# A state-space recurrence turned by its phase for VectorE's scan instruction, and the two sides of SBUF exchanged in the first stage

## The chip, the cores and the metric

The kernel runs on one core of one Trainium2 chip. The metric is the device time of one launch in microseconds, the median of the runs. Three runs of the kernel before took 3642.49, 3650.92 and 3659.8 us. The engines are called as in the profile: PE is TensorE, DVE is VectorE, ACT is ScalarE, POOL is GpSimd, SP is SyncE, which here only issues DMAs. ACT and POOL issue DMAs too, in the order of their own instructions.

## The reference

`reference` computes a first block (three mixers, their output projection and a feed-forward layer) and then a second block of two layers on 256 latent rows `x` and 256 context rows `ctx`, each 1024 wide. Layer 0 applies a chunk mixer and a PEER layer (a product-key lookup of rows of two large tables) to `x` and to `ctx`. Layer 1 applies a state-space mixer to `x`, in which the context takes part, and a PEER layer to `x`. The change lies in the state-space mixer, which is this, cut:

```python
def _diag_scan(a_r, a_i, bu_r, bu_i, h0=None):       # h[t] = a * h[t-1] + bu[t], complex, a is diagonal
    if h0 is not None:
        inj_r, inj_i = _cmul(a_r, a_i, h0[0], h0[1])
        bu_r = bu_r.at[0].add(inj_r)
        bu_i = bu_i.at[0].add(inj_i)
    ...
def _ssm_direction(u_lat, u_ctx, ...):
    hc_r, hc_i = _diag_scan(a_r, a_i, *inject(u_ctx))
    hx_r, hx_i = _diag_scan(a_r, a_i, *inject(u_lat), h0=(hc_r[-1], hc_i[-1]))
    return readout(hx_r, hx_i)
def _ssm_mixer(...):
    mag = exp(lr * step); a_r = mag * cos(li * step); a_i = mag * sin(li * step)
    ...
    y = forward(u_x, u_c) + reversed(backward(u_x[::-1], u_c[::-1]))
    val, gate = split(gelu(y + d_skip * u) @ w_out)
    return val * sigmoid(gate)
```

There is one complex state per group and state index and direction. Only the last state of the context's scan is used; it seeds the scan over the latent rows.

## The kernel before

The program is written in Python, and a scheduler with a simulated timeline sets the order of the instructions on each engine from the data dependences, the sizes of buffers and priorities (`c.low()` marks work that gives way). Tiles of a pool with one side ("left", the default, or "right") are stacked on that side of SBUF; a pool opened later on the same side overlies the memory of one that was closed, and its first writes wait until the last reads there are done.

`tile_block` runs these stages. The prefix (0 to some 345 us) computes four chunks of the modulation (a small matrix product on `cvec`), then side by side the tables of the state-space mixer (`ssm_build`, low priority, pool `sb` on the right), the context's norm and chunk mixer (pool `c0` on the left, with the pool `cm` inside) and the fused keys of layer 0's PEER (`fuse_keys`, pool `fk` on the left; heads 4 to 7 last). After the prefix, pools `sp` and `c1` open on the right (norm of the context for its PEER: the rows `brow`, `nrow` and the token rows `htok`, which POOL adds up), and `b0` on the left for the first block. The context's PEER is gathered row by row by POOL's indirect DMAs under the first block and under the dense PEER layer of `x` (`peer_dense`). Near the end of `peer_dense` the context's half of the state-space mixer runs (`ssm_ctx`), then the latent half (`ssm_mixer`), then layer 1's `peer_dense` and the final norm.

`ssm_build` computes, for 64 state columns on each of 128 partitions, the coefficient a of the state (`ar`, `ai`, from the cosine and sine `hs`, `sn` and the size `mag`), its powers a, a2, a3, a4, then the powers of a4 (call it A) up to the eighth by `cmul` on DVE (six small instructions each, helper `tt`, line 1196), copies of them by ACT into `pt`, and stores `pt` as `ssm_p`. A and its eighth power stay as `A1, A2, B1, B2`. The rest of `ssm_build`, which is left as it is, makes injection matrices `ssm_m`, readout matrices `ssm_g` and within-step matrices `ssm_t` in eight rounds; each round begins with a memset of `ts` by POOL and ends with stores that ACT issues. Because a matrix product takes four time steps at once, 256 rows make 64 steps with coefficient A.

`ssm_inject` multiplies the input by `ssm_m` on PE into four time-series per pair of states (32 pairs, two directions d, real and imaginary r) of 64 steps, copied to `Sx` by ACT. The scan over the 64 steps is then done in three parts: `ssm_local` runs seven steps inside eight blocks of eight (each step four DVE instructions for half a group of pairs, 128 elements per partition), one of four groups on POOL; `ssm_carry` runs seven steps over the blocks; `ssm_apply` (only for the latent rows) multiplies the carried states by the powers in `ssm_p` and adds them, partly on POOL. `ssm_ctx` works on four groups of eight pairs, with loads issued by POOL; `ssm_mixer` likewise, then PE reads out `Hx` with `ssm_g` (line 1598) and `ssm_t` (line 1596).

Lines of helpers: 159 and 166 copy a PSUM bank to SBUF by ACT or DVE, 308 and 315 split a weight tile in two parts by ACT and by DVE or POOL, 227, 251 and 254 are small transposes and row broadcasts on PE, 777 is the matrix product of `peer_dense`, 909 that of `fuse_keys`, 806 and 832 are additions of a modulation and of a residual.

Of the kernel before, what the change touches and what calls it, by code (L numbers as in the profile page):

```python
# [11 lines left out]
F32 = mybir.dt.float32  # L12
# [4 lines left out]
ALU = mybir.AluOpType  # L17
# [1159 lines left out]
def ssm_build(c, pool, sb):  # L1177

    nc, I, tc = c.nc, c.I, c.tc
    A1, A2, B1, B2 = (pool.tile([P, 32, 2, 2], F32, name=n) for n in ("A1", "A2", "B1", "B2"))  # L1180
    pd = c.dram.tile([P, 1024], F32, name="ssm_p")
# [51 lines left out]
    pw = sb.tile([P, 5, 2, W], F32, name="pw")  # L1233
    tt(pw[:, 1, 0], mag, hs, ALU.mult)
    tt(pw[:, 1, 1], mag, sn, ALU.mult)
    ar, ai = pw[:, 1, 0], pw[:, 1, 1]
# [17 lines left out]
    def cmul(ore, oim, xr, xi, yr, yi, w1, w2):  # L1254
        tt(w1, xr, yr, ALU.mult)
        tt(w2, xi, yi, ALU.mult)
        tt(ore, w1, w2, ALU.subtract)
        tt(w1, xr, yi, ALU.mult)
        tt(w2, xi, yr, ALU.mult)
        tt(oim, w1, w2, ALU.add)  # L1260

    for n in (2, 3, 4):
        cmul(pw[:, n, 0], pw[:, n, 1], pw[:, n - 1, 0], pw[:, n - 1, 1], ar, ai, t1, t2)

    pt = sb.tile([P, 32, 2, 2, 8], F32, name="pt")
    nc.gpsimd.memset(pt[:, :, :, :, 0:1], 0.0)
    cur = pw[:, 4]
    for n in range(1, 9):
        if n > 1:
            nx = sb.tile([P, 2, W], F32, tag="pn", name="pn", bufs=2)  # L1270
            cmul(nx[:, 0], nx[:, 1], cur[:, 0], cur[:, 1], pw[:, 4, 0], pw[:, 4, 1], t1, t2)
            cur = nx
        srcs = [cur[:, j].rearrange("p (d q) -> p q d", d=2) for j in range(2)]
        if n < 8:
            for j in range(2):
                nc.scalar.copy(pt[:, :, :, j, n], srcs[j])
        if n in (1, 8):
            X1, X2 = (A1, A2) if n == 1 else (B1, B2)
            for r in range(2):
                nc.scalar.copy(X1[:, :, :, r], srcs[0])  # L1280
                nc.scalar.mul(X2[:, :, :, r], srcs[1], 1.0 - 2.0 * r)
    nc.scalar.dma_start(pd, pt.rearrange("p a d r n -> p (a d r n)"))
# [114 lines left out]
    return dict(a4=(A1, A2), a32=(B1, B2), powers=pd, m=md, g=gd, t=td)  # L1397


def ssm_inject(c, uT, Sx, mats, g, first=0):  # L1400


    for q in range(4 * g, 4 * g + 4):
        m = mats(q).rearrange("p (a j m) -> p a j m", a=2, j=4)
        ps = c.ps()
        for a in range(2):
            for j in range(4):
                c.nc.tensor.matmul(
                    ps[:, (a * 4 + j) * 64 : (a * 4 + j + 1) * 64], m[:, a, j, :], uT[:, 2 * q + a, :], start=True, stop=True
                )  # L1410
        i = 2 * q - first
        c.evac(Sx[:, i : i + 2].rearrange("p a d r j -> p (a d r j)"), ps, eng="a")
# [12 lines left out]
def ssm_local(c, eng, pool, A, Sx, p0, n, tag, first=0):  # L1425

    m = n // 2

    def at(h, j):
        return _view(Sx, (p0 - first + h * m) * 256 + j, [[256, m], [128 + 7 - 2 * j, 2], [64, 2], [8, 8]])

    def step(j, i):

        for h in range(2):
            a = [v[:, p0 + h * m : p0 + (h + 1) * m].unsqueeze(4).to_broadcast([P, m, 2, 2, 8]) for v in A]
            if i < 2:
                t[h][i] = pool.tile([P, m, 2, 2, 8], F32, tag=f"{tag}{i}{h}", name=f"sl{i}", bufs=1)
                eng.tensor_tensor(t[h][i], a[i], at(h, j - 1), ALU.mult)  # L1440
            else:
                v = t[h][0] if i == 2 else _view(t[h][1], 8, [[32, m], [16, 2], [-8, 2], [1, 8]])
                eng.tensor_tensor(at(h, j), at(h, j), v, ALU.add)

    t = [[None, None], [None, None]]
    for j in range(1, 8):
        for i in range(4):
            step(j, i)


def block_view(t, s):

# [12 lines left out]


def ssm_apply(eng, pool, pw, C, Sx, H, p0, n, d, tag):

    shp = [P, n, 2, 8, 7]
    ps = slice(p0, p0 + n)  # L1470
    t1 = pool.tile(shp, F32, tag=tag + "1", name="sa1", bufs=1)
    t2 = pool.tile(shp, F32, tag=tag + "2", name="sa2", bufs=1)
    cb = C[:, ps, d].rearrange("p q r b -> p q (r b)").unsqueeze(3).to_broadcast([P, n, 16, 7])
    for r, t in enumerate((t1, t2)):
        power = _view(pw, p0 * 32 + d * 16 + r * 8 + (1 if d == 0 else 7), [[32, n], [0, 16], [1 - 2 * d, 7]])
        eng.tensor_tensor(t.rearrange("p q r b j -> p q (r b) j"), cb, power, ALU.mult)
    eng.tensor_tensor(t1[:, :, 0], t1[:, :, 0], t2[:, :, 1], ALU.subtract)
    eng.tensor_tensor(t1[:, :, 1], t1[:, :, 1], t2[:, :, 0], ALU.add)
    hv, sv = (t[:, ps, d].rearrange("p q r (b j) -> p q r b j", b=8) for t in (H, Sx))
    o, i = (slice(1, 8), slice(0, 7)) if d == 0 else (slice(0, 7), slice(1, 8))  # L1480
    eng.tensor_tensor(hv[:, :, :, :, o], t1, sv[:, :, :, :, i], ALU.add)


def ssm_ctx(c, mats, modT, ctx, last, pool):
# [3 lines left out]
    hT = pool.tile([P, KD, S], F32, tag="big", name="chT", bufs=2)  # L1488
# [27 lines left out]
    ends = pool.tile([P, 32, 2, 2, 8], F32, name="ends")  # L1516
    for g in range(4):
        Sx = pool.tile([P, 8, 2, 2, 64], F32, tag="big", name="cSx", bufs=2)
        ssm_inject(c, uT, Sx, lambda q: load(mats["m"][q // 4][:, (q % 4) * 1024 : (q % 4 + 1) * 1024]), g, g * 8)
        pool_too = g in CTX_POOL  # L1520
        ssm_local(
            c, nc.gpsimd if pool_too else nc.vector, pool, mats["a4"], Sx, g * 8, 8, "slp" if pool_too else "slv",
            g * 8,
        )
        for d in range(2):
            sv = Sx[:, :, d].rearrange("p q r (b j) -> p q r b j", b=8)
            nc.scalar.copy(ends[:, g * 8 : (g + 1) * 8, d], sv[:, :, :, :, 0 if d else 7])
    cur = block_view(ends, 0)
    for s in range(1, 8):
        nx = last if s == 7 else pool.tile([P, 32, 2, 2], F32, tag="sst", name="sst", bufs=2)  # L1530
        ssm_carry(c, pool, mats["a32"], block_view(ends, s), cur, nx)
        cur = nx


def ssm_mixer(c, mats, modT, x, last, fill, gate):

    nc, I = c.nc, c.I
    with ExitStack() as out:
# [12 lines left out]
        with c.tc.tile_pool(name="sy", bufs=1) as sy:  # L1551
            Sx = sy.tile([P, 32, 2, 2, 64], F32, name="Sx")
# [17 lines left out]
            nc.scalar.dma_start(pw.rearrange("p a d r n -> p (a d r n)"), mats["powers"])  # L1570

            def at_block(s):
                return block_view(C, s)

            nc.vector.tensor_copy(at_block(0), last)
            for s in range(7):
                e = _view(Sx, 8 * s + 7, [[256, 32], [128 + 49 - 16 * s, 2], [64, 2]])
                ssm_carry(c, sz, mats["a32"], e, at_block(s), at_block(s + 1))
            for d in range(2):
                nc.scalar.copy(H[:, :, d].rearrange("p q r (b j) -> p q r b j", b=8)[:, :, :, :, 7 * d], C[:, :, d])  # L1580
# [339 lines left out]
```

## Time and profile before

| | |
|---|---|
| median of 3 runs | 3650.92 us (3642.49 to 3659.8) |
| the profiled execution's own time | 3635.85 us |
| its span (first to last instruction) | 3634.1 us |
| busy in the span | PE 3284.0, DVE 2640.1, ACT 1402.9, POOL 1338.2 us |
| moved by DMA | 940.44 MB, mean 259 GB/s |
| share of the chain that ended last | PE 57%, DVE 21%, DMA 13% |

The profiled execution is 15 us below the median and 7 us below the fastest of the three runs. The prefix and the two state-space stages are read separately, by windows of 20 or 40 us, because the share of busy time over the whole span hides what limits them.

### The profile page before, as it was taken

The numbers are of one execution on the slowest core, as the hardware profiler recorded it, in microseconds if no ns is written. First come the engines' busy times: TensorE is split into PE (matmuls) and PEld (weight loads), VectorE is DVE, ScalarE is ACT, GpSimd is POOL, SyncE is SP. The second block draws the span as 40 slices with busy tenths as digits, with TensorE's granted clock in tenths as the row PEclk, the third lists the DMA queues.
The fourth block names the chain that finished last, engine by engine and source line by source line (L and its number), as shares of the span: only waits on it lengthen the run. The fifth ranks groups of instructions, "written<-read, shape, count | busy, mean of one in ns | idle before, by whom it ended". The sixth has DMA issues, their size and how long they took to land.

```text
span 3634.1 us, 49746 instructions
## 1 busy us (share of the span) xinstructions
PE 3284.0 (90%) x18136; PEld 2665.8 (73%) x18136; DVE 2640.1 (73%) x5276; ACT 1402.9 (39%) x2586; POOL 1338.2 (37%) x1021
## 2 busy tenths in 40 slices
PE   6996987999889988879999999997589999999998
PEld 4775563747437756678899999976477988999987
DVE  5676986555655568878988888859968987555555
ACT  3553222011310023237444544442133475544454
POOL 0000244444334447448544444414444374001000
PEclk9997998999899999999999999998799999999999
DMA  8875778899588988586998888853554466555553
GB/s 304 288 246 185 280 254 312 336 343 338 211 315 333 355 325 277 178 275 206 357 342 329 338 335 330 336 197 109 199 197 174 163 192 238 209 209 209 209 203 116
DMA packets 280485, 940.44 MB, mean 259 GB/s; under 512 B 22944, under 2 KB 136880, under 8 KB 209200
## 3 DMA queue, kind: packets, MB, share of 16 engines
q1 hardware_dynamic: 142560, 608.22, 46.0%
q0 software_dynamic: 77184, 281.05, 21.2%
q10 hardware_dynamic: 60496, 47.99, 4.0%
q8 instruction: 142, 2.33, 0.2%
q14 instruction: 103, 0.84, 0.1%
HBM read 870.60 MB, written 66.58 MB: 258 GB/s over the span
## 4 chain that ended last, share of the span: by engine, by line
PE 57%; DVE 21%; DMA 13%; issue 4%; POOL 3%; ACT 2%; ACTq 1%; DVEq 0%; POOLq 0%; SPq 0%
PE bank L777 18%; PE bank L350 6%; PE bank L349 6%; PE bank L348 6%; DMA gat<-peer_u_rows,idx 5%; DMA gat<-peer_v_rows,idx 5%; PE bank L364 4%; PE bank L357 4%; DVE spl L315 2%; DVE sl L1440 2%; PE bank L909 2%; POOL o L1102 2%; PE bank L1105 1%; PE bank L337 1%; PE bank L335 1%
## 5 line engine op out<-in xcount | busy, mean ns | idle before, releaser
L315 DVE TENSOR_TENSOR spl<-w,sph 128x1024 fp32r<-128x1024 f32 x552 | 701.9, 1273 | 344.0 <-ACT sph L308 341.8
L308 ACT CAST sph<-w 128x1024 fp32r<-128x1024 f32 x632 | 661.9, 1049 | 558.9 <-PE bank L349 372.6
L350 PE MATMUL bank<-hs,spl 128*128 128x256 f32 x2048 | 582.5, 284 | 6.7 <-DVE spl L315 6.7
L348 PE MATMUL bank<-hs,sph 128*128 128x256 f32 x2048 | 581.0, 284 | 2.0 <-DVE mod L806 1.8
L349 PE MATMUL bank<-hs,sph 128*128 128x256 f32 x2048 | 581.0, 284 | 0.0
L1015 DVE CUSTOM_DVE_ANT_0 gat<-gat,htok 128x1024 f32<-128x1024 f32 x256 | 331.7, 1303 | 177.5 <-DMA gat<-peer_u_rows,idx 154.9
L1027 DVE SCALAR_TENSOR_TENSOR pacc<-gat,act,pacc 128x1024 f32<-128x1024 f32 x256 | 333.8, 1304 | 149.9 <-DMA gat<-peer_v_rows,idx 134.4
L348 PEld LDWEIGHTS bank<-hs,sph 128*128 128x128 f32 x2048 | 392.5, 192 | 11.6 <-ACT sph L308 1.9
L350 PEld LDWEIGHTS bank<-hs,spl 128*128 128x128 f32 x2048 | 392.7, 192 | 10.5 <-DVE spl L315 9.3
L349 PEld LDWEIGHTS bank<-hs,sph 128*128 128x128 f32 x2048 | 392.6, 192 | 8.3 <-issue 0.5
L315 POOL TENSOR_TENSOR spl<-w,sph 128x1024 fp32r<-128x1024 f32 x80 | 201.4, 2518 | 453.5 <-ACT sph L308 436.3
L364 PE MATMUL bank<-hT,w 128*128 128x256 f32 x1472 | 328.6, 384 | 14.1 <-DVE cv L509 8.4
L364 PEld LDWEIGHTS bank<-hT,w 128*128 128x128 f32 x1472 | 283.3, 193 | 64.9 <-issue 11.6
L777 PE MATMUL bank<-sph,wsl 128*128 128x512 f32 x1024 | 318.6, 392 | 2.3 <-DVE wsl L315 2.2
L1000 POOL DMA_INDIRECT gat<-peer_v_rows,idx x176 | 214.2, 1217 | 286.5 <-PE bank L357 61.2
L777 PE MATMUL bank<-spl,wsh 128*128 128x512 f32 x1024 | 319.4, 393 | 0.1
L777 PE MATMUL bank<-sph,wsh 128*128 128x512 f32 x1024 | 307.5, 394 | 2.4 <-ACT wsh L308 2.4
L1000 POOL DMA_INDIRECT gat<-peer_u_rows,idx x176 | 219.1, 1245 | 227.5 <-DVE act L1015 77.9
L357 PE MATMUL bank<-w,hT 128*128 128x512 f32 x576 | 255.6, 603 | 2.2 <-ACT sg L432 2.2
L777 PEld LDWEIGHTS bank<-sph,wsl 128*128 128x128 f32 x1024 | 192.2, 188 | 45.3 <-DVE wsl L315 2.6
L777 PEld LDWEIGHTS bank<-spl,wsh 128*128 128x128 f32 x1024 | 189.8, 188 | 39.8 <-DVE spl L315 0.3
L357 PEld LDWEIGHTS bank<-w,hT 128*128 128x128 f32 x576 | 110.7, 194 | 135.9 <-issue 132.0
(444 smaller groups left out, 5730.3 us busy)
## 6 DMA issues: line engine op xcount, KB each, us to landing
w<-peer_u_t SPq DMA_DIRECT2D x128, 1024.0 KB, 5.6
w<-peer_v_t SPq DMA_DIRECT2D x128, 1024.0 KB, 5.1
w<-ada_w_t SPq DMA_DIRECT2D x48, 1024.0 KB, 6.7
w<-wq_t SPq DMA_DIRECT2D x32, 1024.0 KB, 5.4
w<-w_in_t SPq DMA_DIRECT2D x32, 1024.0 KB, 7.9
gspill<-gstg SPq DMA_DIRECT2D x32, 896.0 KB, 4.6
gq<-gspill SPq DMA_DIRECT2D x28, 1024.0 KB, 6.2
w<-wqk SPq DMA_DIRECT2D x24, 1024.0 KB, 5.3
```

The source lines that it names most:

```text
L308: nc.scalar.copy(hi, src)
L315: eng.tensor_tensor(lo, src, hi.bitcast(F32), ALU.subtract)
L348: mm(ps, wh[:, ks], hh[:, k, :], start=k == 0, stop=False)
L349: mm(ps, wh[:, ks], hl[:, k, :], start=False, stop=False)
L350: mm(ps, wl[:, ks], hh[:, k, :], start=False, stop=k == KD - 1)
L357: m = self.nc.tensor.matmul(outs[t], hT[:, k, t * P : (t + 1) * P], w[k], start=k == 0, stop=k == KD - 1)
L364: m = self.nc.tensor.matmul(ps, block[:, k * P : (k + 1) * P], hT[:, k, :], start=k == 0, stop=k == KD - 1)
L777: c.nc.tensor.matmul(acc[t][cc], a[:, ts_], b[:, cc * 512 : (cc + 1) * 512], start=first and j == 0, stop=last and j == 2,)
L909: nc.tensor.matmul(ps[:, b * P : (b + 1) * P], wv[:, kt, k * P : (k + 1) * P], ks[:, kt, :], start=kt == 0, stop=kt == 1,)
L1000: g = nc.gpsimd.indirect_dma_start(out=gt, out_offset=None, in_=tab, in_offset=bass.IndirectOffsetOnAxis(ap=idx[:, t, s : s + 1], axis=0))
L1015: use = nc.vector.tensor_tensor_reduce(out=gt, in0=gt, in1=h[:, t, :], scale=1.0, scalar=0.0, op0=ALU.mult, op1=ALU.add, accum_out=act[:, ...
L1027: use = nc.vector.scalar_tensor_tensor(acc, gt, act[:, t, s : s + 1], acc, ALU.mult, ALU.add)
```

## The change

**The scan.** The coefficient A of a state is written as its size times a turn, M exp(i w). A state series multiplied at step n by exp(-i w n) obeys a recurrence whose coefficient is the real number M, and that is what VectorE's `tensor_tensor_scan` computes along a row. `ssm_build` makes tables of the phases exp(i w n), n = 0 to 63, for eight groups of four pairs: `square` doubles the angle seven times, and `phases` fills a table in six levels by multiplying what is there with the next doubling; all of it runs on POOL, and ACT issues the store of each table (512 KB). The powers, their copies and `B1, B2` are gone. In `ssm_ctx` and `ssm_mixer`, `ssm_turn` multiplies a group by the conjugate phase (two DVE instructions, two more for sum and difference), four scans follow, and the mixer turns the result back (`ssm_turn` again and four instructions into `Hx`). `ssm_decay` makes the row of M with zeros at the starts (ACT copies, POOL memset). POOL does no other part of the scan. `ssm_ctx` goes in eight groups of four pairs, `ssm_mixer` in four of eight, and in the latter the modulation's later chunks (`fill`) are issued ahead of the scans.

**The sides.** In the prefix `sb` goes to the left, and `c0` with `cm` to the right. So `sp` and `c1` overlie `c0`, and `b0` overlies `sb` and `fk`.

The diff, cut (`ssm_local`, `ssm_carry` and `ssm_apply` are removed whole):

```diff
 def ssm_build(c, pool, sb):
-    for n in (2, 3, 4):
-        cmul(pw[:, n, 0], pw[:, n, 1], pw[:, n - 1, 0], pw[:, n - 1, 1], ar, ai, t1, t2)
...
-    for n in range(1, 9):
-        if n > 1:
...
-            cmul(nx[:, 0], nx[:, 1], cur[:, 0], cur[:, 1], pw[:, 4, 0], pw[:, 4, 1], t1, t2)
...
-    nc.scalar.dma_start(pd, pt.rearrange("p a d r n -> p (a d r n)"))
+    def square(o, cs, si):
+        gp.tensor_tensor(g1, cs, cs, ALU.mult)
+        gp.tensor_tensor(g2, si, si, ALU.mult)
+        gp.tensor_tensor(o[:, 0], g1, g2, ALU.subtract)
+        gp.tensor_tensor(g1, cs, si, ALU.mult)
+        gp.tensor_tensor(o[:, 1], g1, g1, ALU.add)
+
+    square(lv[:, 1], hs, sn)
+    square(lv[:, 0], lv[:, 1, 0], lv[:, 1, 1])
+    for l in range(1, 6):
+        square(lv[:, l], lv[:, l - 1, 0], lv[:, l - 1, 1])
...
+    def phases(k):
+
+        ph = sb.tile([P, 2, 2, 4, 64], F32, tag="ph", name="ph")
+        w = sb.tile([P, 2, 4, 32], F32, tag="phw", name="phw")
+        for cs in range(2):
+            gp.memset(_view(ph, cs * 512, [[256 + 63, 2], [64, 4]]), 1.0 - cs)
+        for l in range(6):
+            L = 1 << l
...
+            for cs in range(2):
+                gp.tensor_tensor(dst[cs], src[0], m[cs], ALU.mult)
+                gp.tensor_tensor(wv, src[1], m[1 - cs], ALU.mult)
+                gp.tensor_tensor(dst[cs], dst[cs], wv, ALU.add if cs else ALU.subtract)
+        nc.scalar.dma_start(pd[k], ph.rearrange("p s d a n -> p (s d a n)"))
+
+    for k in range(8):
+        phases(k)
...
+def ssm_turn(nc, pool, ph, S, n):
+
+    w1, w2 = (pool.tile([P, 2, 2, n * 64], F32, tag=f"sw{i}", name=f"sw{i}") for i in range(2))
+    cs, si = (_view(ph, i * n * 128, [[n * 64, 2], [0, 2], [1, n * 64]]) for i in range(2))
+    nc.vector.tensor_tensor(w1, S.rearrange("p d r a j -> p d r (a j)"), cs, ALU.mult)
+    nc.vector.tensor_tensor(w2, _view(S, n * 64, [[n * 128, 2], [-n * 64, 2], [1, n * 64]]), si, ALU.mult)
+    return w1, w2
...
+def ssm_scan(c, pool, ph, dec, S, n, ini=None):
...
+    w1, w2 = ssm_turn(nc, pool, ph, S, n)
+    flat = S.rearrange("p d r a j -> p d r (a j)")
+    for r in range(2):
+        nc.vector.tensor_tensor(flat[:, :, r], w1[:, :, r], w2[:, :, r], ALU.subtract if r else ALU.add)
+    if ini is not None:
+        o = edge(S, n, False)
+        nc.vector.tensor_tensor(o, o, ini.rearrange("p a d r -> p d r a"), ALU.add)
+    N = n * 64
+    for d in range(2):
+        for r in range(2):
+            s = _view(S, (d * 2 + r) * N + d * (N - 1), [[1 - 2 * d, N]])
+            f = _view(dec, d * N + d * (N - 1), [[1 - 2 * d, N]])
+            nc.vector.tensor_tensor_scan(s, f, s, 0.0, ALU.mult, ALU.add)
...
 def ssm_ctx(c, mats, modT, ctx, last, pool):
+    for h in range(8):
+        p0 = h * 4
+        S_ = pool.tile([P, 2, 2, 4, 64], F32, tag="cSx", name="cSx", bufs=2)
+        ssm_inject(c, uT, S_, lambda q: load(mats["m"][q // 4][:, (q % 4) * 1024 : (q % 4 + 1) * 1024]), p0, 4)
+        ph = load(mats["phase"][h], "cph")
+        ssm_scan(c, pool, ph, ssm_decay(c, pool, mats["m4"], p0, 4), S_, 4)
...
 def ssm_mixer(c, mats, modT, x, last, fill, gate):
+            Sg = {g: inject(g) for g in range(3)}
+            fill(sy)
...
+            for g in range(4):
+                ph = sy.tile([P, 4, 8, 64], F32, tag="ph", name="ph", bufs=2)
...
+                ssm_scan(c, sy, ph, ssm_decay(c, sy, mats["m4"], 8 * g, 8), S_, 8, ini[:, gs])
+
+                w1, w2 = ssm_turn(nc, sy, ph, S_, 8)
+                if g == 0:
+                    Sg[3] = inject(3)
+                H = sy.tile([P, 2, 2, 8, 64], F32, tag="Hx", name="Hx", bufs=2)
...
-    with tc.tile_pool(name="sb", bufs=1, side="right") as sb:
+    with tc.tile_pool(name="sb", bufs=1) as sb:
-        with tc.tile_pool(name="fk", bufs=1) as fk, tc.tile_pool(name="c0", bufs=1) as p:
+        with tc.tile_pool(name="fk", bufs=1) as fk, tc.tile_pool(name="c0", bufs=1, side="right") as p:
-            chunk_mixer(c, p, ch3, xc, lambda g: gate_bcast(c, mod0, 1, 0, g), mid)
+            chunk_mixer(c, p, ch3, xc, lambda g: gate_bcast(c, mod0, 1, 0, g), mid, "right")
```

Line numbers of the kernel after are 3 lower for helpers, and some 18 higher in the rest of `ssm_build`.

ACT's queue in the prefix, the kernel after, at the stores of the seventh and eighth phase table (`ssm_p<-ph`); `mst` and `wqk` belong to the fused key of head 4, `sph<-w` is a split of a weight of the context's chunk mixer:

```order
L156 COPY rep<-mt 128x4x128 x2
L1297 DMA ssm_p<-ph 128x1024
L305 CAST sph<-w 128x1024 x3
L156 COPY mst<-bank_65 128x512
L912 DMA wqk_2008<-mst 128x4x128
L191 ACTIVATE half,ss<-xc 128x512 x2
L912 DMA wqk_2008<-mst 128x4x128
L1297 DMA ssm_p<-ph 128x1024
L156 COPY mst<-bank_62 128x512
```

The kernel before has one store of `ssm_p` in the prefix, and none at this place; ACT's instructions behind each store stand behind POOL's work for that table.

POOL's queue in the prefix, the kernel after, at the end of the seventh table and the beginning of the eighth (`ts` is the memset with which a round of `ssm_build` begins):

```order
L1295 TENSOR_TENSOR phw<-ph,lv 128x256
L1296 TENSOR_TENSOR ph<-ph,phw 128x2x4x32
L1364 MEMSET ts 128x512
L1286 MEMSET ph 128x2x4 x2
L1294 TENSOR_TENSOR ph<-ph,lv 128x2x4 x2
L1295 TENSOR_TENSOR phw<-ph,lv 128x8
L1296 TENSOR_TENSOR ph<-ph,phw 128x2x4
```

The kernel before, the same queue:

```order
L1286 MEMSET mt 128x2048
L1287 MEMSET gb 128x2560
L1346 MEMSET ts 128x512 x8
L1686 ISA
L1686 TENSOR_TENSOR htok<-half,brow 128x512 x4
```

Before, the eight memsets of `ts` stand alone ahead of `htok`; after, 323 multiplications and additions of `square` and `phases` stand among them, and the last two memsets and `htok` behind all of these.

PE's queue at the end of layer 0's `peer_dense`, first before (injections of the context, line 1408, among the last matrix products, line 777):

```order
L777 MATMUL bank_63<-sph,wsl 128x512
L1408 MATMUL bank_68<-cuT,cw 128x64 x8
L1408 MATMUL bank_62<-cuT,cw 128x64 x8
L777 MATMUL bank_64<-sph,wsl 128x512
L777 MATMUL bank_65<-sph,wsh 128x512
L777 MATMUL bank_61<-sph,wsh 128x512
```

and after:

```order
L774 MATMUL bank_65<-sph,wsl 128x512
L1426 MATMUL bank_68<-cuT,cw 128x64 x8
L1426 MATMUL bank_62<-cuT,cw 128x64 x8
L774 MATMUL bank_61<-sph,wsl 128x512
L224 MATMUL bank_66<-ident,mod_105 128x128 x4
L1426 MATMUL bank_68<-cuT,cw 128x64 x8
```

Before, five such pairs of injections stand ahead of the last product of `peer_dense`; after, one pair does and the other seven stand behind it.

DVE's queue in `ssm_ctx`, the kernel after, one group (line 1481 is the scan, four of 256 elements):

```order
L1461 TENSOR_TENSOR sw_11448<-cSx,cph 128x1024
L1462 TENSOR_TENSOR sw_11449<-cSx,cph 128x1024
L193 TENSOR_TENSOR s_18532<-ss 128x2
L1472 TENSOR_TENSOR cSx<-sw_11448,sw_11449 128x2x256 x2
L174 TENSOR_SCALAR rstd<-s_18532 128x2
L1481 SCALAR_TENSOR_TENSOR cSx<-dec,cSx 128x256 x4
```

Eight such groups take the place of 168 instructions of the local scan and 28 of the carry on DVE.

## Rows read from the trace of the kernel before

**Rows 1.** Busy time of the span, from the page.

```profile
PE 3284.0 (90%) x18136; PEld 2665.8 (73%) x18136; DVE 2640.1 (73%) x5276; ACT 1402.9 (39%) x2586; POOL 1338.2 (37%) x1021
```

**Rows 2.** Windows of the prefix: busy us (count), granted clock, DMA share, GB/s.

```profile
160.00:200.00 40.00, 38.31 (x233) 22.44 (x232) 18.08 (x49) 16.61 (x45) 0.00 (x0) 0.93 0.93 363
200.00:240.00 40.00, 36.84 (x213) 29.71 (x213) 31.80 (x69) 20.60 (x44) 1.05 (x2) 0.94 0.53 186
```

**Rows 3.** Timeline of ACT: start, us, instruction, idle before and releaser.

```profile
42.35 0.24 ACT L1230 ACTIVATE hs<-s 128x64 f32<-128x64 f32 x1
247.59 0.59 ACT L159 COPY mst<-bank 128x512 f32<-128x512 f32 x1 [7.84 <-PE bank L909]
338.19 0.34 ACTq L1396 DMA_DIRECT2D ssm_t<-ts  x1
341.39 0.59 ACT L159 COPY brow<-bank 128x512 f32<-128x512 f32 x1 [8.80 <-DMA ssm_t<-ts]
```

**Rows 4.** Timeline of PE at the same place.

```profile
342.03 5.49 PE L251 MATMUL bank<-mod,ident 128*128 128x512 f32 x6 [6.47 <-ACT brow L159]
```

**Rows 5.** Landing of the stores and loads of ssm_p.

```profile
DMA to landing us min/median/max: 7.5/8.5/9.4
```

**Rows 6.** POOL instructions: ns of one, least, median, most.

```profile
L1440 POOL TENSOR_TENSOR sl<-A,cSx x28: 456/610/4684, 2460.6 to 2501.5; 128x128 f32<-128x128 f32 x28
L963 POOL TENSOR_TENSOR eq<-eq,cid x48: 1852/1890/3007, 393.7 to 2904.2; 128x864 f32<-128x864 f32 x48
L1102 POOL TENSOR_SCALAR o<-iota,slots x160: 780/1127/3721, 1600.7 to 3019.3; 128x128 f32<-128x128 f32 x160
```

**Rows 7.** Timeline of POOL and DVE in the routing stage.

```profile
400.65 1.04 DVE L959 TENSOR_TENSOR eq<-ti,iota 128x864 f32<-128x864 f32 x1
401.84 1.88 POOL L963 TENSOR_TENSOR eq<-eq,cid 128x864 f32<-128x864 f32 x1 [2.69 <-DVE eq L959]
402.35 2.28 DVE L959 TENSOR_TENSOR eq<-ti,iota 128x864 f32<-128x864 f32 x1
```

**Rows 8.** DVE in the prefix by form: count, busy us, mean ns of one.

```profile
L315 DVE TENSOR_TENSOR spl<-w,sph 128x1024 fp32r<-128x1024 f32 x24 | 29.1, 1221 | 8.1 <-ACT sph L308 7.9
L1309 DVE TENSOR_TENSOR pb<-w,w 128x256 f32<-128x256 f32 x45 | 18.9, 421 | 10.5 <-ACT mt L1320 9.9
L832 DVE TENSOR_TENSOR xc<-xc,half 128x512 f32<-128x512 f32 x4 | 2.6, 684 | 0.0
L1196 DVE TENSOR_TENSOR s<-pn,pw 128x64 f32<-128x64 f32 x24 | 4.3, 220 | 0.1
```

**Rows 9.** Windows of the state-space stages.

```profile
2560.00:2580.00 20.00, 17.55 (x155) 14.46 (x154) 19.79 (x53) 6.72 (x12) 19.64 (x18) 1.00 0.92 352
2449.10:2674.40 225.30, 151.77 (x1042) 131.31 (x1041) 219.24 (x481) 47.63 (x78) 123.12 (x159) 0.83 0.44 157
```

**Rows 10.** The same of the instructions of local scan (tile sl) alone.

```profile
2440.00:2700.00 260.00, 136.87 (x336) 77.52 (x112) 0.84 0.46 167
```

**Rows 11.** The same of the instructions of carry (tile st) alone.

```profile
2440.00:2700.00 260.00, 17.89 (x56) 0.84 0.46 167
```

**Rows 12.** The same of the instructions of apply (tile sa) alone.

```profile
2440.00:2700.00 260.00, 43.11 (x45) 37.72 (x35) 0.84 0.46 167
```

**Rows 13.** Timeline of PE at the ends of peer_dense and of the readout.

```profile
2467.68 3.68 PE L1408 MATMUL bank<-cuT,cw 128*128 128x64 f32 x32
2472.40 0.63 PE L777 MATMUL bank<-sph,wsl 128*128 128x512 f32 x2
2680.50 0.38 PE L1596 MATMUL bank<-w,suT 128*64 128x128 f32 x2
2680.72 1.04 PE L1598 MATMUL bank<-w,Hx 128*64 128x128 f32 x8
2681.69 2.20 PE L1609 MATMUL bank<-ident,sy 64*128 64x64 f32 x32
```

**Rows 14.** Timeline of DVE at the last apply.

```profile
2673.76 0.62 DVE L1481 TENSOR_TENSOR Hx<-sa,Sx 128x448 f32<-128x448 f32 x1
```

More of the change, by code (lines that the diff above doesn't have):

```diff
@@ L1179, in ssm_build @@
     nc, I, tc = c.nc, c.I, c.tc
-    A1, A2, B1, B2 = (pool.tile([P, 32, 2, 2], F32, name=n) for n in ("A1", "A2", "B1", "B2"))
-    pd = c.dram.tile([P, 1024], F32, name="ssm_p")
+    A1, A2 = (pool.tile([P, 32, 2, 2], F32, name=n) for n in ("A1", "A2"))
+    M4 = pool.tile([P, 32, 2], F32, name="M4")
+    pd = c.dram.tile([8, P, 1024], F32, name="ssm_p")
     md = c.dram.tile([NS // 2, P, NP * 1024], F32, name="ssm_m")
@@ L1232, in ssm_build @@
     nc.vector.tensor_scalar(hs, hs, -2.0, 1.0, ALU.mult, ALU.add)
[L1233 to L1236, printed above, removed]
+    ar, ai = small("ar"), small("ai")
+    tt(ar, mag, hs, ALU.mult)
+    tt(ai, mag, sn, ALU.mult)
     den, am1 = small("den"), small("am1")
@@ L1396, in ssm_build, with ssm_inject @@
         nc.scalar.dma_start(td[:, q * NP * P : (q + 1) * NP * P], ts_.rearrange("p a t m -> p (a t m)"))
-    return dict(a4=(A1, A2), a32=(B1, B2), powers=pd, m=md, g=gd, t=td)
-def ssm_inject(c, uT, Sx, mats, g, first=0):
-    for q in range(4 * g, 4 * g + 4):
+    return dict(a4=(A1, A2), m4=M4, phase=pd, m=md, g=gd, t=td)
+def ssm_inject(c, uT, S, mats, p0, n):
+    for i in range(0, n, 2):
+        q = (p0 + i) // 2
         m = mats(q).rearrange("p (a j m) -> p a j m", a=2, j=4)
@@ L1467, in ssm_apply, with edge @@
[L1467 to L1481, printed above, removed]
+def edge(S, n, last):
+    i = 63 if last else 0
+    return _view(S, i, [[2 * n * 64 + 63 - 2 * i, 2], [n * 64, 2], [64, n]])
@@ L1515, in ssm_ctx @@
             nc.vector.transpose(uT[:, cc * 16 : (cc + 1) * 16, t * 32 : (t + 1) * 32], u)
[L1516 to L1523, printed above, removed]
-        )
[L1525 to L1532, printed above, removed]
+    ends = pool.tile([P, 32, 2, 2], F32, name="ends")
+    eph = pool.tile([P, 2, 32, 2], F32, name="eph")
+    for h in range(8):
[4 more added lines that the diff above has]
+        ssm_scan(c, pool, ph, ssm_decay(c, pool, mats["m4"], p0, 4), S_, 4)
+        nc.scalar.copy(ends[:, p0 : p0 + 4].rearrange("p a d r -> p d r a"), edge(S_, 4, True))
+        for i in range(2):
+            nc.scalar.copy(
+                eph[:, i, p0 : p0 + 4].rearrange("p a d -> p d a"), _view(ph, i * 512 + 63, [[256 - 63, 2], [64, 4]])
+            )
+    t1, t2 = (pool.tile([P, 32, 2, 2], F32, name=f"st{i}") for i in range(2))
+    for t, i in ((t1, 0), (t2, 1)):
+        nc.vector.tensor_tensor(t, ends, eph[:, i].unsqueeze(3).to_broadcast([P, 32, 2, 2]), ALU.mult)
+    for r in range(2):
+        nc.vector.tensor_tensor(
+            last[:, :, :, r], t1[:, :, :, r], t2[:, :, :, 1 - r], ALU.add if r else ALU.subtract
+        )
 def ssm_mixer(c, mats, modT, x, last, fill, gate):
@@ L1570, in ssm_mixer @@
[L1570 to L1580, printed above, removed]
@@ L1583, in ssm_mixer @@
+            nc.vector.tensor_tensor(ini, ini, _view(t2, 1, [[4, 32], [2, 2], [-1, 2]]), ALU.add)
+            y = sz.tile([64, 4, D], F32, name="sy")
             yv = y.rearrange("p t (q m) -> p q t m", m=32)
             tm = c.w(mats["t"], 32)
[L1585 to L1601 removed]
@@ new lines, in ssm_mixer @@
+            for g in range(4):
+                gs = slice(8 * g, 8 * g + 8)
+                ph = sy.tile([P, 4, 8, 64], F32, tag="ph", name="ph", bufs=2)
+                for h in range(2):
+                    nc.scalar.dma_start(
+                        ph[:, :, 4 * h : 4 * h + 4], mats["phase"][2 * g + h].rearrange("p (s a n) -> p s a n", s=4, a=4)
+                    )
+                S_ = Sg.pop(g)
+                ssm_scan(c, sy, ph, ssm_decay(c, sy, mats["m4"], 8 * g, 8), S_, 8, ini[:, gs])
[3 more added lines that the diff above has]
+                H = sy.tile([P, 2, 2, 8, 64], F32, tag="Hx", name="Hx", bufs=2)
+                nc.scalar.copy(edge(H, 8, False), last[:, gs].rearrange("p a d r -> p d r a"))
+                for d in range(2):
+                    for r in range(2):
+                        o, i = (slice(1, 64), slice(0, 63)) if d == 0 else (slice(0, 63), slice(1, 64))
+                        v1, v2 = (w[:, d, r].rearrange("p (a j) -> p a j", a=8)[:, :, i] for w in (w1, w2))
+                        nc.vector.tensor_tensor(H[:, d, r, :, o], v1, v2, ALU.add if r else ALU.subtract)
+                for q in (2 * g, 2 * g + 1):
+                    ps = c.ps()
+                    gm = c.w(mats["g"][q], 2, NP * 512).tiles[0].rearrange("p (a j m) -> p a j m", a=NP, j=4)
+                    for a in range(NP):
+                        pr = q * NP + a
+                        o = ps[:64, a * P : (a + 1) * P]
+                        nc.tensor.matmul(o, uT[:, pr, :], tm[pr], start=True, stop=False)
+                        for j in range(4):
+                            nc.tensor.matmul(
+                                o, H[:, j // 2, j % 2, pr - 8 * g, :], gm[:, a, j, :], start=False, stop=j == 3
+                            )
+                    nc.scalar.activation(
+                        yv[:, q * NP : (q + 1) * NP], ps[:64].rearrange("p (a t m) -> p a t m", a=NP, t=4),
+                        AF.Gelu_apprx_tanh,
+                    )
```

127 lines of the change are left out of this document (42 added, 85 removed).

## The prediction

> **What bounds the kernel now.** I read the page first: PE is busy in 90% of the span and DVE in 73% [rows 1], so over most of the span DVE hides under PE. The reader is to see in the windows that this doesn't hold in the two stretches that the change touches.
>
> In the state-space stages, 2449.1 to 2674.4 us, DVE is busy 219 of 225 us and PE 152 [rows 9]. The recurrence is most of it: 136.9 us of DVE for the local scans [rows 10], 17.9 for the carry [rows 11], 43.1 for the apply [rows 12], 197.9 in all. The remaining 21 us are splits of weights, norms and transposes. PE's readout ends 7.3 us behind DVE's last apply, at 2681.7 [rows 13, 14]. DVE bounds this stretch, and POOL takes a fourth of the scan beside it.
>
> In the prefix no engine is full: DVE 18 to 32 of 40 us, PE 37 to 38, DMA up to 363 GB/s, POOL nothing but memsets [rows 2]. It is a chain over PE, ACT, DVE and stores. At its end ACT's `brow` waits for the last store of `ssm_t`, issued at 338.19, and PE has then stood 6.47 us [rows 3, 4].
>
> **The change in the state-space stages.** A context group has two instructions of 1024 elements, two of 512 and four scans of 256; a mixer group twice two of 2048, two of 1024, four scans of 512, and four of 504. An instruction of two operands in SBUF takes 0.42 us for 256 elements, 0.684 for 512, 1.22 for 1024 [rows 8]. From the last two the slope is 1.05 ns an element, so 2048 take some 2.3 us (an estimate).
>
> What one scan costs no row shows. From below it is such an instruction of its size, 0.42 and 0.684; nothing in it could take less, since it reads and writes the same elements. From above I take an element more of that slope for each element, 0.42 + 0.27 = 0.69 and 0.684 + 0.54 = 1.22. I take the upper end, since each element needs the result of the one before it, which none of these rows has to wait for.
>
> - Context, 8 groups: 2 x 1.22 + 2 x 0.684 + 4 x 0.69 = 6.6 us, 53 in all (44 at the lower end).
> - Mixer, 4 groups: 4 x 2.3 + 2 x 1.22 + 4 x 1.22 + 4 x 0.684 + 0.2 for the start values = 19.5 us, 78 in all (69).
>
> That is 131 us (113) for 197.9: 67 us of DVE gone (85).
>
> [...]
>
> What is given back:
> - In PE's order five pairs of injections stand ahead of the end of `peer_dense` before, and one after. So `peer_dense` ends four of 3.68 us earlier, at 2473 - 15 = 2458 [rows 13], but DVE's first turn can start only there and not at 2449. Some of DVE's other work ahead of it moves earlier too; I count 8 us.
> - The readout of the last group is two quarters of four pairs, at most 8 x 1.42 = 11.4 us [rows 13], where 7.3 now lie behind the last apply: 2 to 4 us. That of groups 0 to 2 lies beside DVE's 19 us for the next group.
> - DMA: 12 MB for the context (8 of matrices, 4 of phases) at 1.5 MB per 6.6 us is 238 GB/s; then phases 4, matrices 8, `ssm_t` 2, `ssm_g` 8 and the modulation 8 MB within some 90 us is 350 GB/s, and the fastest window here has 352 [rows 9]. The modulation stands ahead of `ssm_t` and `ssm_g` on SP's queue, so group 0's readout can come late, and with two buffers of `Hx` DVE would wait for it. I count 5 us, and up to 30 as a bound.
>
> ACT's part (evacuations, `dec`) is a few short copies a group beside DVE's 6.6 us, and POOL, which was busy 123 us here [rows 9], keeps only memsets. So 67 - 8 - 3 - 5 = 51 us are won.
>
> **The change in the prefix.** DVE loses 10 `cmul`, 60 instructions of 0.22 us or less [rows 8], 8 to 13 us, beside other work. POOL gains 323 instructions in one chain: 35 of 64 elements and 8 tables of 6 each at 8, 16, ..., 256 elements.
>
> A POOL instruction takes 0.456 us for 128 elements at the least and 1.852 for 864 [rows 6]: 1.9 ns an element and 0.21 us fixed. A table is then 36 x 0.21 + 6 x 504 x 0.0019 = 13.3 us, `square` 35 x 0.33 = 11.7, together 118 us. Beside a working DVE 128 elements have a median of 0.61 [rows 6], 1.34 times: 158 us. Each table but the last is one buffer whose store must have landed, 8.5 us for 512 KB [rows 5], before the next begins: 60 us. `hs` and `sn` are there at 42.35 [rows 3] and DVE's normalisation takes to some 47. The chain ends at 47 + 158 + 60 = 265 us. Its bounds: 47 + 118 + 50 = 215, and, if each of them took as long over its least as line 1102 does with 128 elements (1.127 to 0.456, 2.5 times [rows 6]), 47 + 290 + 60 = 397.
>
> What waits for it is in ACT's order: the seventh and eighth store stand just around the first `mst` of the fused keys, whose counterpart began at 247.59 [rows 3]. ACT executes in order, so behind the waiting store are queued the copies `mst` that feed PE's line 909, the splits and all later copies of `ssm_build`. At 265 ACT waits some 20 us there (0 at 215, 150 at 397). I put the prefix's delay at 20 us.
>
> Two things beside it. In the routing stage one DVE instruction that takes 1.04 us alone took 2.28 when a POOL instruction was under way, and ended with nothing in between [rows 7]. The prefix has some 160 such DVE instructions with both operands in SBUF (24 of line 315, and 45 each of line 1309 and of its two sisters 1305 and 1308, 29 + 3 x 19 = 86 us [rows 8]), so DVE loses too; its idle time of 8 to 22 us in 40 [rows 2] takes up most of it, and I count 6 us. [...]
>
> The exchange: `c1` no longer waits for `ssm_build`'s memory, so the 6.47 us of PE [rows 4] can go. `brow` is still issued behind `ssm_build`'s last instructions on DVE and ACT, so nothing more than that can. Now `b0` waits for `ssm_build` instead, but its tiles are first written behind the context's norm, so that this is covered.
>
> Prefix: +20 + 6 - 6 = 20 us later. PE's work behind it is a chain through the whole span, so this is not made up.
>
> **Sum.** 20 - 51 = -31 us. Against the profiled execution's 3636 us that is 3605; the median of the runs stands 15 above, so the prediction is 3619 us.
>
> **Rivals.**
>
> 1. *POOL's chain becomes the prefix's bound* and the change is slower. Place: ACT's stores of the phase tables. Price: each us by which the chain ends behind 247 us is a us of delay, up to 150. It decides from where POOL's instructions take 0.75 us in the mean (323 x 0.75 + 60 + 47 = 349, delay 100): then +100 - 51 = +49, 3700 us; from 80 us of delay the gain is gone to beyond 0.5%. For it: the median beside DVE is a third above the least, single ones took 4.7 us [rows 6], and the tables are built from rows of 1 to 32 elements, which no row of POOL shows. Against it: three quarters of the instructions have 64 elements or fewer.
>
> 2. *The scans cost no more than a product*, and the phase chain is done in time. 85 - 16 = 69 won, the prefix at -6 to 0: 3580 us. For it: the bound from below; against it: the dependence from element to element.
>
> 3. *The loads and the hand-overs take the gain.* Phases double what each group waits for; if readout and turns run at the pace of the loads and the whole 30 us are lost, 51 - 25 = 26 are won and the prefix gives 20 back: 3645 us, no change. For it: 350 GB/s needed where the best window has 352 [rows 9]; against it: loads of earlier stages can be ahead.
>
> That the exchange does nothing, because the order keeps `brow` where it was, costs 6 us in each of these.
>
> **How the numbers follow.** The forecast (3595 to 3640) has 0.48, rival 1 0.17, rival 2 0.13, rival 3 0.22. A difference of under 0.5%, 18 us, can't be told from none here; the limits are 3633 and 3669. Faster: 0.85 of the forecast, all of rival 2, 0.3 of rival 3: 0.41 + 0.13 + 0.07 = 0.61. Same: 0.07 + 0.15 + 0.02 of rival 1 = 0.24. Slower: the rest of rival 1, 0.15. The range 3572 to 3672 leaves out most of rival 1 and the far end of rival 2, some 0.2; that of the forecast alone is 3595 to 3640.
>
> **What would show it.** Steps right: the eighth store of `ssm_p` near 265 us with ACT idle ahead of it for POOL; `brow` near 360; DVE rows of scans of 0.69 and 1.22 us; DVE at 19 of 20 us from 2480 on; the readout's end 30 us earlier than 2682. Wrong: POOL's small instructions over 0.7 us (rival 1) or the chain done by 215; scans of 0.42 and 0.68 (rival 2); DVE idle in the mixer behind DMAs or PE (rival 3).

## The result, and the profile after

| | before | after | ratio, 95% interval |
|---|---|---|---|
| first comparison, 4 runs each | 3646.70 us | 3584.79 us | 0.9826 [0.9801, 0.9851] |
| second, 9 and 5 runs | 3643.26 us | 3594.56 us | 0.9853 [0.9825, 0.988] |

The forecast was 3619 us. The change made the kernel 49 to 62 us faster, where 31 were forecast.

Single profiled executions differ by 20 us in the middle, which the change doesn't touch. So I cut every execution at four marks: PE's first product of the first block (`hT`), of layer 0's dense weights (`wsl`), the last transpose of the readout (`sy`), and the span's end.

| us | prefix | first block on | dense weights to readout | rest | span |
|---|---|---|---|---|---|
| before | 438.4 | 1285.1 | 960.2 | 950.4 | 3634.1 |
| before, again | 433.4 | 1296.0 | 967.0 | 949.9 | 3646.3 |
| sides alone | 429.4 | 1282.9 | 965.5 | 950.2 | 3628.0 |
| before without powers | 428.8 | 1293.1 | 966.4 | 951.3 | 3639.6 |
| after | 427.1 | 1279.0 | 914.0 | 953.0 | 3573.1 |
| after, again | 433.5 | 1294.3 | 919.5 | 953.0 | 3600.3 |
| after, third | 430.1 | 1290.9 | 922.6 | 953.2 | 3596.8 |
| scan alone | 425.7 | 1296.4 | 917.7 | 950.3 | 3590.1 |
| after without phase levels | 429.5 | 1285.0 | 914.1 | 950.3 | 3578.9 |
| phase levels twice | 476.7 | 1281.3 | 915.3 | 950.2 | 3623.5 |
| phases early | 432.3 | 1287.2 | 910.1 | 951.4 | 3581.0 |
| fill late | 428.3 | 1293.5 | 911.9 | 952.4 | 3586.1 |
| both | 424.7 | 1283.6 | 908.1 | 951.7 | 3568.1 |
| both, sides as before | 428.1 | 1299.0 | 902.6 | 949.7 | 3579.4 |

The four kernels with the old scan have a mean of 964.8 us in the third stretch, the six with the new one and the mixer as changed (after to phase levels twice) 917.2: -47.6, where -51 were predicted. The prefix of before has a mean of 435.9 (two executions), of after 430.2 (three): -5.7, where +20 were predicted. Executions of one kernel differ there by 5 to 6 us, so the table shows that the prefix is not later; that it is earlier is not shown beyond that scatter.

**The scan.** Rows of DVE by form (count, busy us, mean ns, idle before) in the kernel after:

```profile
L1481 DVE TENSOR_TENSOR_SCAN cSx<-dec,cSx 128x256 f32<-128x256 f32 x32 | 19.5, 668 | 0.0
L1461 DVE TENSOR_TENSOR sw<-Sx,ph 128x2048 f32<-128x2048 f32 x8 | 18.3, 2292 | 11.6 <-DMA ph<-ssm_p 11.2
L1481 DVE TENSOR_TENSOR_SCAN Sx<-dec,Sx 128x512 f32<-128x512 f32 x16 | 18.3, 1205 | 0.4
L1472 DVE TENSOR_TENSOR cSx<-sw,sw 128x512 f32<-128x512 f32 x16 | 10.3, 684 | 0.0
L1598 DVE TENSOR_TENSOR Hx<-sw,sw 128x504 f32<-128x504 f32 x16 | 9.8, 677 | 9.5 <-ACT Hx L1593 9.3
L1461 DVE TENSOR_TENSOR sw<-cSx,cph 128x1024 f32<-128x1024 f32 x8 | 9.6, 1201 | 4.3 <-ACT cSx L156 4.3
```

With L1462 (18.3 and 9.7) and L1472 of the mixer (9.4) the recurrence takes 123 us of DVE, where [rows 10 to 12] had 198. Two stalls stand in this list, 11.2 and 9.3 us. Windows of the same stretch (busy of PE, PEld, DVE, ACT, POOL, then clock, DMA share, GB/s):

```profile
2480.00:2500.00 20.00, 18.31 (x117) 16.02 (x116) 20.00 (x28) 9.44 (x23) 1.47 (x6) 1.00 0.33 106
2500.00:2520.00 20.00, 20.00 (x126) 17.87 (x125) 11.24 (x21) 8.17 (x15) 0.13 (x1) 1.00 0.67 214
2520.00:2540.00 20.00, 15.47 (x138) 13.89 (x137) 13.38 (x10) 5.21 (x10) 0.13 (x1) 1.00 1.02 404
2560.00:2580.00 20.00, 16.06 (x75) 15.95 (x76) 19.77 (x19) 3.69 (x7) 0.13 (x1) 0.53 0.63 243
```

DVE is full in the first and last. Between 2500 and 2540 it works for 24.6 of 40 us, and in the second half of that DMA runs at 404 GB/s, above the 352 of [rows 9]. SP's queue and PE's timeline show who comes first there (start, us, instruction):

```profile
2519.35 29.68 SPq L61 DMA_DIRECT2D w<-ada_w_t  x8
2550.41 3.46 SPq L61 DMA_DIRECT2D w<-ssm_t  x2
```

```profile
2440.36 0.48 PE L774 MATMUL bank<-sph,wsl 128*128 128x512 f32 x1
2565.66 13.89 PE L1426 MATMUL bank<-suT,w 128*128 128x64 f32 x64
2579.49 0.69 PE L1605 MATMUL bank<-w,suT 128*64 128x128 f32 x2
2618.89 1.46 PE L1621 MATMUL bank<-ident,sy 64*128 64x64 f32 x16
```

The modulation's weights stand ahead of `ssm_t`. The injections of the last group follow, and only then the first readout, so both `Hx` buffers stay full and DVE waits the 9.3 us. Still, from the last product of `peer_dense` to the readout's last transposes (start to start) it is 178 us, where [rows 13] had 209; and `peer_dense`, with fewer injections ahead, ends 734 us after its `wsl` mark instead of 749.

**The prefix.** ACT and PE, rows that answer to [rows 3, 4]:

```profile
260.70 0.34 ACTq L1297 DMA_DIRECT2D ssm_p<-ph  x1
261.14 0.59 ACT L156 COPY mst<-bank 128x512 f32<-128x512 f32 x1 [11.86 <-POOL ph L1296]
319.21 0.34 ACTq L1414 DMA_DIRECT2D ssm_t<-ts  x1
331.35 0.59 ACT L156 COPY brow<-bank 128x512 f32<-128x512 f32 x1 [7.88 <-DMA gbi<-gate_bias]
```

```profile
331.99 2.93 PE L248 MATMUL bank<-mod,ident 128*128 128x512 f32 x3 [5.44 <-ACT brow L156]
```

The eighth store of `ssm_p` stands at 260.70 (265 predicted), and ACT stood idle for 11.9 us just there (20 predicted). But `brow` is 10 us earlier than before, not 20 later. POOL ended that wait, but PE's products for the same copy `mst` (line 906) ended only a little before:

```profile
255.94 3.84 PE L906 MATMUL bank<-ks,w 128*128 128x128 f32 x32
```

These 32 records fill the two PSUM banks of this copy and the next. Without POOL the copy could have begun when its bank was full, by an estimate from this row at 258 us if it is the first and 259.8 if the second, and not 11.9 us earlier: POOL held it by some 1.4 to 3.1 us. POOL's chain by form:

```profile
L1296 POOL TENSOR_TENSOR ph<-ph,phw 128x256 f32<-128x256 f32 x16 | 12.9, 804 | 1.3
L1296 POOL TENSOR_TENSOR ph<-ph,phw 128x64 f32<-128x64 f32 x16 | 8.2, 510 | 0.6
L1296 POOL TENSOR_TENSOR ph<-ph,phw 128x8 f32<-128x8 f32 x16 | 4.6, 289 | 0.5
L1286 POOL MEMSET ph<- 128x8 f32 x16 | 1.2, 115 | 49.2 <-DMA ssm_p<-ph 48.9 <-POOLq L1786 0.3
```

The last row holds the seven waits for a table's store, 49 us, where the sum had 60. The sum lacks another wait: the memsets of `ts` stand in the same queue, and between 40 and 261 us two of them waited for stores of the rounds:

```profile
POOL ts L1364 <- DMA ssm_t<-ts: 12.0, 2, 9.1
```

### The profile page after: what moved, and what is told of

It is laid out like the page before. It is cut to its first block, busy times and chain, and to the rows that moved or that the text cites. A ratio compares the mean times of both kernels' runs of the same rounds, so it can differ in the third digit from the quotient of the medians.

```text
span 3573.1 us, 49682 instructions
## 1 busy us (share of the span) xinstructions
PE 3281.0 (92%) x18136; PEld 2668.2 (75%) x18136; DVE 2577.0 (72%) x4922; ACT 1406.8 (39%) x2606; POOL 1365.2 (38%) x1232
## 5 line engine op out<-in xcount | busy, mean ns | idle before, releaser
L305 ACT CAST wsh<-pw 128x256 fp32r<-128x256 f32 x256 | 104.2, 408 | 272.1 <-PE bank L774 268.5
```

The source lines that it names most:

```text
L305: nc.scalar.copy(hi, src)
```

## Experiments: the prefix

**Sides alone** (the kernel before with the sides exchanged).

```diff
-    with tc.tile_pool(name="sb", bufs=1, side="right") as sb:
+    with tc.tile_pool(name="sb", bufs=1) as sb:
...
-        with ... tc.tile_pool(name="c0", bufs=1) as p:
+        with ... tc.tile_pool(name="c0", bufs=1, side="right") as p:
...
```

> The kernel before with only the sides of SBUF exchanged. Theory A (the prefix ended 10 us earlier in the kernel after because ssm_build lost its 60 power instructions at its head, so its eight rounds run earlier; the exchange hardly matters): the last ssm_t store stays near 338 us, brow starts at 336 to 342, the time is 0 to 5 us shorter. Rival B (the exchange did it: brow no longer waits for the stores of ssm_build): brow near 331, the time 10 to 17 us shorter.

3639.75 us, ratio 0.9974 [0.9958, 0.999]; `brow` at 332.96. The time lies between the two theories.

**Scan alone** (the kernel after with the sides as before: the diff above, reversed).

> The kernel after with the sides as before, so that only the scan is changed. Theory A: the last ssm_t store is near 319 us as in the kernel after, brow 325 to 333, the time 55 to 65 us shorter than before. Rival B: brow falls back to 338 to 342, the time is only 42 to 50 us shorter.

3579.25 us, ratio 0.9811 [0.9792, 0.9831]; `brow` at 326.09. Theory A held. The scan change is all that can be measured of the gain: the exchange on top of it gives nothing, though it gives 0.26% alone. The two don't add.

**Before without the powers.** Left out: A's powers; copies of other values stand in their place.

```diff
-    for n in (2, 3, 4):
+    for n in ():
...
-        if n < 8:
+        if n < 2:
```

> The kernel before without the powers of the coefficient (the ten cmul of ssm_build and twelve of its copies by ACT are left out, so the blocks are combined with wrong powers); the scan stays as it was. Theory A: the rounds' stores of ssm_t come 9 to 36 us earlier as in the kernel after, the last near 319, brow 328 to 336, the time 6 to 15 us shorter. Rival B: the last store at 333 to 338, the time within 4 us of before. The state-space stage itself (2449 to 2682 us less the prefix's gain) is the same for both.

3632.79 us, ratio 0.9972 [0.9952, 0.9992]; `brow` at 332.05, but the last `ssm_t` store at 329.97, where after has 319.21. So that the missing powers advance the rounds holds for a part at most. This kernel and the one with the sides alone gain the same, 0.28 and 0.26%, and have the same prefix in the table, 428.8 and 429.4 us. All that the two share is an order other than that of before. So it may be that order, and neither the sides nor the powers, that cost before some 0.3%; no run tests this by itself.

**After without the phase levels.** Left out: the six levels; the tables hold 0.5.

```diff
+        gp.memset(ph, 0.5)
-        for l in range(6):
+        for l in range(0):
```

> The kernel after with the phase tables left unbuilt: the six levels of phases are left out (a memset stands for them), the squares and the stores stay; the states are then turned by a wrong phase. Theory A (POOL's chain of 270 us lies beside the rounds and costs nearly nothing): ACT's wait of 11.9 us ahead of the second mst goes, brow 322 to 331, the time 0 to 8 us shorter than the kernel after, 60 to 70 shorter than before. Rival C (as the prediction had it, the chain holds ACT and slows DVE by 26 us): brow near 305, the time 20 to 30 us shorter than the kernel after.

3585.21 us, ratio 0.9834 [0.9814, 0.9854]; `brow` at 334.10. The time is that of theory A, but `brow` didn't come earlier. POOL's chain costs nothing that can be measured, though ACT waits for it. The copies `mst` show why: the two around the eighth store begin 14.4 us apart in after, and 14.5 apart here, where ACT's idle time ahead of the second, 4.5 us, ends with PE's products and not with POOL: they take that step anyway, as the row of line 906 showed for after. What the chain does cost lies on DVE; one line of 256-element products and the whole window from 47 to 261 us, after and then this kernel:

```profile
L1327 DVE TENSOR_TENSOR pb<-w,w 128x256 f32<-128x256 f32 x50 | 23.9, 479 | 3.6 <-ACT mt L1338 1.3 <-ACT gb L1338 0.8
47.00:261.00 214.00, 190.33 (x1170) 152.33 (x1168) 172.29 (x383) 119.62 (x305) 140.81 (x342) 0.95 0.79 276
```

```profile
L1328 DVE TENSOR_TENSOR pb<-w,w 128x256 f32<-128x256 f32 x49 | 20.9, 426 | 7.4 <-ACT mt L1339 5.8
47.00:261.00 214.00, 185.09 (x1119) 149.71 (x1118) 157.42 (x364) 117.64 (x303) 22.56 (x58) 0.93 0.76 268
```

Beside POOL the product is 12% longer (0.479 to 0.426 us), and [rows 8] had 0.421. DVE's whole busy time there is 172.3 to 157.4 us. Of these 15 us some 7 are 19 instructions more that fall into the window in after (383 to 364); instruction for instruction the stretch is some 8 us, where 6 were counted, and the time shows nothing of them: DVE is idle there for 41.7 of the 214 us.

**Phase levels twice.**

```diff
-        for l in range(6):
+        for l in [*range(6), *range(6)]:
```

> The kernel after with the six levels of every phase table computed twice (same result), so that POOL's chain has 288 instructions more, some 150 us. Theory A (the chain is beside the rounds and the fused keys, and only matters once ACT waits at its stores for longer than the slack of the prefix): the eighth store of ssm_p comes at 390 to 420 instead of 261, ACT stands for most of the difference, brow moves from 331 to 400 to 440, the time is 60 to 110 us longer than the kernel after. Theory D (the prefix does not hang on the phase tables at all): brow stays within 10 us of 331.

3626.79 us, ratio 0.9942 [0.9918, 0.9967]. ACT:

```profile
377.76 0.34 ACTq L1297 DMA_DIRECT2D ssm_p<-ph  x1
380.57 0.59 ACT L156 COPY brow<-bank 128x512 f32<-128x512 f32 x1 [43.80 <-DMA ssm_p<-ph]
```

In the three profiles of after the eighth store stands at 262.8 us in the mean (260.7, 263.7, 263.9) and `brow` at 334.3 (331.4, 337.3, 334.3). Here the chain ends 115 us later and `brow` comes 46 later, ACT having stood 43.8 us for the last store; the time is 32 to 42 us longer than after. So rival 1 is a real mechanism, as theory A says, at less than the sizes expected: 69 of the 115 us did not count, and the point lies at a chain's end of some 332 us and not of 247.

That slack belongs to this program's own order. The scheduler knows of the longer chain, and put the last two stores behind all the fused keys, just ahead of `brow`, where in after seven copies `mst` of ACT stand behind the eighth store. How late the chain may end with the order of after kept isn't shown by any run.

**Both kernels once more**, and after in five rounds.

> The kernel before, unchanged, profiled once more on another execution. Theory A (its order has two long fused-key steps that belong to the order): the first brow of ACT stands again at 341 us, within 2 us, with the ssm_t stores of 288.5, 319.5 and 338.2 within 2 us. Theory B (an execution's scatter): brow falls between 326 and 335 as in every other kernel. The time itself is to stay at 3635 to 3660 us by either.

> The changed kernel, unchanged, profiled once more. Theory A: brow at 331.4 us again, within 2 us. Theory B: it scatters by 5 us or more. The stretch from the first state-space weights' step to the last output transpose is to be 914 us again within 3 us; the time 3575 to 3590 us.

> The changed kernel, unchanged, against the kernel before in more rounds. The profiles put the change at -49 us in the stretch from layer 0's dense weights to the readout and -6 in the prefix (means of several kernels), -1 to +3 behind it. Theory A (that is all of it): ratio 0.985, 3595 us where before has 3650. Theory B (the first comparison's -62 us is right, and 8 to 10 us lie in the middle, hidden by its scatter of 17 us): 0.9826.

Before: 3648.12 us and `brow` at 336.44; after: 3602.10 and 337.29; then 3594.56 and 334.28. So `brow` scatters by 5 to 6 us in either, which in before lies between the two theories and in after is theory B, and the 10 us of the first two profiles are 4.6 in the means, no more than that scatter. The time of after in the second of these runs lies above the 3575 to 3590 expected; the third is as its theory A has it. What repeats is the order's pattern: two steps between copies `mst` near 276 and 302 us take 16.8 and 20.1 us in before and 16.8 and 19.9 again, and no other kernel here has both. Why that order stalls there, and the others don't, I didn't settle. The second ratio lies nearer to the sum of the stretches, -48 - 6 + 3.

## Experiments: the mixer

**Phases early**: the tables of the first two groups are loaded ahead, in the outer pool.

```diff
...
+            phs = {g: phase(g) for g in range(2)}
...
+                ph = phs.pop(g) if g in phs else phase(g)
```

> The kernel after with the phase tables of the mixer's first two groups loaded ahead, before the latent norm (in the pool sx, by ACT's queue). Theory E (DVE's 11.2 us of waiting for ph at 2515 to 2526 is a price of the mixer): DVE's first turn of the mixer starts 8 to 12 us earlier, but the readout of group 0 still waits for ssm_t and the last two ssm_m behind the modulation's eight loads, so that only 0 to 6 us of time are won. Theory F (the wait hides nothing else): 9 to 12 us shorter than the kernel after.

**Fill late**: the modulation behind the second group.

```diff
-            fill(sy)
...
+                if g == 1:
+                    fill(sy)
```

> The kernel after with the modulation's later chunks (fill) issued after the mixer's second group instead of ahead of the scans. Theory E (group 0's readout starts at 2579.5, 37 us after its states are there, because ssm_t, the last ssm_m and ssm_g are loaded behind the modulation's 8 MB): PE's readout starts 15 to 25 us earlier in the stage, DVE's 9.3 us wait for Hx goes, and the modulation's 9 us of PE move into the readout; 4 to 12 us shorter than the kernel after. Theory F (loads are the bound, whatever their order): within 3 us.

**Both**, and both with the sides as before:

> Both e6_ph_early and e7_fill_late. Theory E: DVE works from the end of the context's scan to the last Hx with under 5 us of waiting, the readout ends 15 to 22 us earlier in the stage, 12 to 20 us shorter than the kernel after. Theory F: no shorter than the better of the two alone.

> The changed kernel with the two edits of the mixer (phase tables of groups 0 and 1 loaded early, modulation's fill behind group 1) and the sides of SBUF as before. Theory: the mixer's -6 us stay, the exchange gives nothing on top of the scan, so the time is that of the kernel with both edits and the sides exchanged, 3565 to 3580 us, ratio 0.979; where the exchange still matters it would be 5 us or more above that.

Phases early: 3583.94 us, 0.9809 [0.9778, 0.9839]; of the wait of 11.2 us one of 4.8 for `Sx` is left, that of `Hx` stays (9.7). Fill late: 3588.36, 0.9837 [0.9805, 0.9869]; the wait of `Hx` goes, and DVE waits 8.4 us for the modulation's products and 8.4 for `Sx` where the 11.2 stood. The interval of neither is clear of those of after. Both: 3573.76, 0.9792 [0.9761, 0.9822]; with the sides as before 3575.36, 0.9803 [0.9777, 0.9829], beside 3594.56 of after on the same chip. In the first of the two this wait of DVE (total us, times, longest) stands where the 11.2 us stood, and none for `Hx`:

```profile
DVE sw L1461 <- ACT Sx L156: 4.8, 1, 4.8
```

The third stretch is 908.1 and 902.6 us where after has 914.0 to 922.6, so some 13 us (means) of what DVE won had gone into the two stalls, as theory E says. These two are the fastest kernels here, and again the sides make no difference that can be measured.

## Why the prediction was right and wrong

*The recurrence on DVE* was right. Scans took 0.668 and 1.205 us (0.69 and 1.22 taken), the turns 2.29 (2.3). The upper end was the right choice: 1.205 - 0.668 = 0.537 us for 256 more elements are 2.1 ns each, twice the 1.05 that [rows 8] give for a product. That the dependence from element to element is the cause was the author's argument; no run shows it.

*Given back there*: 75 us fewer on DVE where 67 were counted, 48 won, so 27 were given back where 16 were counted. That 48 lies so near to 51 is in part luck: the two errors cancel. The term of 5 us for the DMAs was mis-sized; it measured 11.2 + 9.3 us of waiting, and some 13 us came back when both waits were removed. It is rival 3's mechanism, at two thirds of its price. The 15 us of injections behind `peer_dense` came as worked out.

*The prefix, "+20 + 6 - 6 = 20 us later"*, is the step that failed: the prefix measured -5.7 us. What failed is the rule that turned the chain's end into time, that each us by which it ends behind 247 us is a us of delay. The prediction put the wait of an in-order engine down as delay without asking what else the queued copies had to wait for. The copy behind the eighth store had to wait for PE's products until 258 to 259.8 us anyway, so that of the 11.9 us only 1.4 to 3.1 were POOL's; without the chain `brow` comes no earlier (334.10, where after has 334.3 in the mean). The 6 us of DVE were some 8, and cost nothing either that can be measured. Why the prefix of before has its two long steps stays open.

The chain's end itself, 261 for 265, was met partly by luck: POOL was busy for 141 us from 47 to 261, memsets included, where 158 were counted, the stores took 49 and not 60, and 12 us of waiting for the rounds' stores weren't in the sum. In rival 1, 227 of the 323 instructions have 64 elements or fewer, 70% and not three quarters, which changes nothing.

*DVE beside POOL*: the one pair of [rows 7] had 2.28 us for 1.04. In the prefix the effect was smaller, 0.479 us for 0.426 in the mean of the products of line 1327, 12%.

*The exchange*: 6 us were counted, 0.26% (some 9 us) is what it gave alone, and beside the scan nothing. In the prediction's own terms, with the prefix at -6 the sum is -57, inside what the two comparisons show; the range held the time.

## What to carry to other kernels

A wait that you find, or foresee, on an in-order engine is a delay only if what stands behind it is not late for another reason: look at when everything else that it needs is there, which here stood in one row of PE (of ACT's 11.9 us some 1.4 to 3.1, by the estimate above, were POOL's). Doubling the suspected work shows whether the wait can ever decide; but where a scheduler makes the order anew, the point that it gives is that of the new order. A linear recurrence with complex coefficients becomes a real scan by turns of phase; here, where DVE was the bound, it took 48 us off the stretch, and some 13 more with the loads of its tables put ahead of it and other loads behind. Cut executions at marks before comparing them: a stretch that the change doesn't touch moved by more than a term of the sum.

## What the runs showed of the hardware

POOL's products and sums of 8 to 32 elements in `phases` take nearly the same, 0.29 to 0.34 us (means by line); those of 64 take 0.39 to 0.52 and those of 256 0.71 to 0.80. So in this chain the instructions of 8 to 32 elements were paid by their count. A scan on DVE took 0.668 us for 256 elements and 1.205 for 512, 2.1 ns for each further element; a product took 1.201 us for 1024 and 2.292 for 2048, 1.07 ns. Beside POOL's chain DVE's products of 256 elements of line 1327 took 0.479 us in the mean, and 0.426 without it. The second of the four stretches, the same work in all kernels, took between 1279 and 1299 us.
